# Expert stage: weight splits and gate products moved from GpSimd to VectorE, gates built by one float32 one-hot matmul per token

## The chip, the core and the metric

The kernel runs on one core of a Trainium2 chip. The metric is the device time of one execution in microseconds; shown is the median over several executions. The engines are called PE (TensorE's matmuls), DVE (VectorE), ACT (ScalarE), POOL (GpSimd) and SP (SyncE, which issues most of the transfers), as in the profile.

## The reference, cut to what matters

Two transformer blocks run one after the other over 512 tokens of width 1024. The second one ends in a feed-forward of 16384 experts, of which every token takes 16 in each of 8 heads. The change lies in this last part alone:

```python
def peer_ffn(x, wq, sub_keys, u_tab, v_tab):
    ...
    q = (xf @ wq).reshape(t, PEER_HEADS, 2, PEER_DKEY // 2)
    scores = jnp.einsum("thpc,hpnc->thpn", q, sub_keys).astype(jnp.float32)
    s_top, i_top = lax.top_k(scores, PEER_TOPK)
    cand_s = (s_top[:, :, 0, :, None] + s_top[:, :, 1, None, :]).reshape(t, PEER_HEADS, PEER_TOPK * PEER_TOPK)
    ...
    best_s, best_pos = lax.top_k(cand_s, PEER_TOPK)
    expert_idx = jnp.take_along_axis(cand_i, best_pos, axis=-1)
    gates = jax.nn.softmax(best_s, axis=-1)
    ...
        u = jnp.take(u_tab, ec, axis=0)
        act = jax.nn.gelu(jnp.einsum("cd,chkd->chk", xc, u).astype(jnp.float32)) * gc
        vv = jnp.take(v_tab, ec, axis=0)
        return jnp.einsum("chk,chkd->cd", act.astype(vv.dtype), vv)
```

An expert's number is i1 * 128 + i2, where i1 and i2 are places in two lists of 128 sub-keys.

## The kernel before

Everything is kept as [channel, token] tiles. A float32 product is made of three PE matmuls in the faster float32r type (`mm3`, L262 to L264): each operand is split into a high part, which ACT makes (`wh`, L249), and a low part, the difference, which is one subtraction on DVE or, if a caller says so, on POOL (`wl`, L250, in `unit`). A weight unit is [128, 1024] and comes by one transfer of 512 KB that SP issues (L246); there are four buffers for raw units and three for split ones.

`peer` does the expert stage. The experts of the first 128 tokens are gathered row by row: an indirect transfer that POOL issues (L1705), then one DVE instruction per row (L1689 for the dot product, L1697 for the weighted sum of the second table). For the other 384 tokens all 16384 experts are applied. The **first product** runs over 128 units of 128 experts, `j` in `range(NE)`: `proj` against the unit's columns of the first table (24 matmuls of 384 columns), then GELU on ACT (`hg`, L1758), then a transfer of the activations to DRAM (`HS`, L1759). In the units of the first product two generators are stepped in fixed rates: `route` (1.65 steps per unit) and `chosen`, the gathered rows. `route` first ranks: 16 query projections, scores against the sub-keys (plain float32 matmuls, L1576), the 16 largest by DVE (`top16`, L1506 to L1510), and `resolve`, which finds the sub-key numbers by one-hot products (equality on DVE at L1545, product on POOL at L1548, sum on DVE at L1551). Then it builds gates: for the 384 tokens, in six blocks of 64, four tokens at a time (96 such steps). Per step it makes a one-hot of i1 (`o1`, L1637) and of i2 (`o2`, L1639) on DVE and the i2 one-hot times the gate (`og`); a matmul per token multiplies them, and the [128 i1, 128 i2] result of each token goes from PSUM into `st`. Since the one-hot product is in float32r, the gate is split in two: `og` has a high half by ACT (four instructions, L1644) and a low half by POOL (L1641), the matmul has 256 columns (L1651), and the two halves are added as ACT copies the first into `st` (L1655) and DVE adds the second (L1656). A finished block goes to DRAM (`G`, L1669), the last stays in `st`.

The low half of the weights is made by POOL in every unit while the ranking is not done (`self.known < P`), and in every second one after that.

The **second product** has again 128 units, and `weighted(j)` prepares each: a weight unit of the second table, and for every pair of units the activations (`hs`, 384 KB, L1778) and gates (`gs`, 320 KB, L1780) from DRAM, both in tiles of the pool `four`, which has four. POOL multiplies them (`hg`, L1785 for the five blocks in `gs`, L1787 for the one in `st`), ACT and DVE split the product (`yh` L257, `yl` L258), and PE does 24 matmuls into eight PSUM banks. SP issues its transfers in one queue, in order; a transfer into a tile waits for the last reader of what was there.

A scheduler fixes each engine's order of instructions when the program is built; every engine then works through its own list, and an instruction that waits holds up all behind it.

## Time and profile before

| | |
|---|---|
| runs | 3840.15 us median of 3 (3839.1 to 3840.55) |
| span of the profiled execution | 3839.7 us |
| PE busy | 3588.0 us (93%) |
| DVE busy | 2635.3 us (69%) |
| ACT busy | 1529.3 us (40%) |
| POOL busy | 1204.1 us (31%) |
| granted PE clock, mean | 0.968 |

The profile is of one execution, and its span goes from the first to the last instruction; no other time of that execution is recorded, so the span is its own time here. An engine's busy time is the sum of its instructions' spans, and an instruction's span includes what it is held up by after it has started. The shares are means over a program of many stages. The expert stage is the last third: the first product from about 2430 us to 3264 us (ranking up to 2747 us, gates after that), the second from 3264 us to 3785 us.

### The profile page before, as it was taken

To read this page: it belongs to the slowest core of one execution; us is meant where nothing else is said; L and a number is where in the kernel's file an instruction comes from. 1 tells how busy PE (TensorE), PEld (TensorE's weight loads), DVE (VectorE), ACT (ScalarE), POOL (GpSimd) and SP (SyncE) were. 2 spreads that over 40 slices of the span, in tenths; PEclk is the share of its full clock that TensorE was granted. 3 is DMA by queue.
4 is the path that set the end of the run, shared out by engine and by line. 5 is a ranking of instruction groups with operands and counts; after the bars stand their busy time and mean duration, and the time that the engine had idled before them with its cause. 6 is when DMAs were issued, how large, how long until landed. Compare 5 with 4: busy or idle time off the path is not lost. (4 is left out here: it accounts for less than half of the span.)

```text
span 3839.7 us, 50675 instructions
## 1 busy us (share of the span) xinstructions
PE 3588.0 (93%) x18665; PEld 3119.2 (81%) x18665; DVE 2635.3 (69%) x4580; ACT 1529.3 (40%) x2746; POOL 1204.1 (31%) x987
## 2 busy tenths in 40 slices
PE   6999999999999999999999989899788888999996
PEld 4888876788888888767888877788788888999996
DVE  7555587655563324776332485689998999999997
ACT  3222366422232223564322353433356466333332
POOL 4000310100010002101000132466676676766664
PEclk9999999999999999999999999999899899999998
DMA  7566320266643333301333222476676777999994
GB/s 232 175 181 198 107 92 17 71 204 192 198 159 99 94 95 109 106 17 45 99 94 95 84 77 69 142 228 222 187 249 236 237 241 255 352 340 336 345 339 142
DMA packets 230329, 648.92 MB, mean 169 GB/s; under 512 B 22784, under 2 KB 80304, under 8 KB 227520
## 3 DMA queue, kind: packets, MB, share of 16 engines
q1 hardware_dynamic: 190592, 506.20, 40.6%
q0 software_dynamic: 39488, 139.48, 10.8%
q8 instruction: 146, 2.39, 0.3%
q14 instruction: 103, 0.84, 0.1%
HBM read 597.36 MB, written 48.23 MB: 168 GB/s over the span
## 5 line engine op out<-in xcount | busy, mean ns | idle before, releaser
L264 PE MATMUL proj<-yh,wl 128*128 128x512 f32 (+2 forms) x3296 | 1214.4, 370 | 52.9 <-DVE wl L250 33.7
L249 ACT ACTIVATE wh<-raw 128x1024 fp32r<-128x1024 f32 (+2 forms) x622 | 648.2, 1043 | 1446.8 <-PE proj L263 796.1
L262 PE MATMUL proj<-yh,wh 128*128 128x512 f32 (+2 forms) x3296 | 1204.3, 370 | 19.2 <-DVE cc L1455 8.8
L263 PE MATMUL proj<-yl,wh 128*128 128x512 f32 (+2 forms) x3296 | 1212.4, 369 | 7.9 <-DVE yl L380 3.9
L250 DVE TENSOR_TENSOR wl<-raw,wh 128x1024 fp32r<-128x1024 f32 (+2 forms) x527 | 707.3, 1343 | 500.8 <-ACT wh L249 495.5
L264 PEld LDWEIGHTS proj<-yh,wl 128*128 128x128 f32 x3296 | 635.4, 193 | 141.9 <-DVE wl L250 42.0
L262 PEld LDWEIGHTS proj<-yh,wh 128*128 128x128 f32 x3296 | 630.2, 193 | 107.9 <-DVE cc L1455 8.9
L263 PEld LDWEIGHTS proj<-yl,wh 128*128 128x128 f32 x3296 | 635.0, 193 | 92.9 <-DVE yl L380 7.3
L393 POOL TENSOR_TENSOR acc<-acc,sq 128x512 f32<-128x512 f32 x32 | 48.0, 1498 | 1482.2 <-ACT sq L392 1132.6
L262 PE MATMUL acc<-yh,wh 128*128 128x384 f32 x1024 | 344.5, 337 | 0.4 <-ACT yh L257 0.4
L263 PE MATMUL acc<-yl,wh 128*128 128x384 f32 x1024 | 344.4, 336 | 0.1
L264 PE MATMUL acc<-yh,wl 128*128 128x384 f32 x1024 | 343.9, 336 | 0.5 <-DVE wl L250 0.5
L264 PE MATMUL proj<-gh,wl 128*128 128x512 f32 (+1 forms) x792 | 293.2, 370 | 0.8 <-DVE wl L250 0.8
L262 PE MATMUL proj<-gh,wh 128*128 128x512 f32 (+1 forms) x792 | 292.9, 370 | 0.0
L263 PE MATMUL proj<-gl,wh 128*128 128x512 f32 (+1 forms) x792 | 292.8, 370 | 0.0
L250 POOL TENSOR_TENSOR wl<-raw,wh 128x1024 fp32r<-128x1024 f32 x95 | 240.8, 2538 | 100.3 <-ACT wh L249 99.7
L518 DVE SCALAR_TENSOR_TENSOR scr<-raw,cact 128x1024 bf16<-128x1024 f32 x128 | 161.9, 1265 | 160.6 <-DMA raw<-in_wada 160.0
L1705 POOL DMA_INDIRECT row<-in_purows,c x128 | 150.7, 1177 | 194.3 <-DVE row L1689 121.3
L1697 DVE SCALAR_TENSOR_TENSOR vacc<-row,act,vacc 128x1024 f32<-128x1024 f32 x127 | 208.8, 1644 | 0.4
L1689 DVE SCALAR_TENSOR_TENSOR row<-row,cact 128x1024 f32<-128x1024 f32 x128 | 196.7, 1549 | 11.0 <-DMA row<-in_purows,c 10.8
L1705 POOL DMA_INDIRECT row<-in_pv,c x128 | 149.9, 1171 | 158.3 <-DVE vacc L1697 69.7
L262 PEld LDWEIGHTS acc<-yh,wh 128*128 128x128 f32 x1024 | 192.4, 188 | 1.0 <-ACT yh L257 0.7
(432 smaller groups left out, 5176.6 us busy)
## 6 DMA issues: line engine op xcount, KB each, us to landing
raw<-in_wada SPq DMA_DIRECT2D x144, 512.0 KB
raw<-in_pu SPq DMA_DIRECT2D x128, 512.0 KB
raw<-in_pv SPq DMA_DIRECT2D x128, 512.0 KB
raw<-in_wg SPq DMA_DIRECT2D x84, 512.0 KB
raw<-in_wu SPq DMA_DIRECT2D x84, 512.0 KB
raw<-in_wd SPq DMA_DIRECT2D x64, 512.0 KB
acts<-hg SPq DMA_DIRECT2D x128, 192.0 KB
hs<-acts SPq DMA_DIRECT2D x64, 384.0 KB
```

The costliest lines, as they stand in the source:

```text
L249: nc.scalar.activation(h[:, :n], raw[:, :n], AF.Copy)
L250: ins = (engine or nc.vector).tensor_sub(l[:, :n], raw[:, :n], h[:, :n].bitcast(F32))
L262: mm(out, lhsT=lh, rhs=rh, start=start, stop=False)
L263: mm(out, lhsT=lh, rhs=rl, start=False, stop=False)
L264: mm(out, lhsT=ll, rhs=rh, start=False, stop=stop)
L393: (engine or nc.vector).tensor_add(acc[:, s], acc[:, s], sq)
L518: nc.vector.scalar_tensor_tensor(scr, raw, 1.0, self.cact, op0=OP.mult, op1=OP.mult, accum_out=self.mod[:, l, j:j + 1])
L1689: nc.vector.scalar_tensor_tensor(row, row, 1.0, XN, op0=OP.mult, op1=OP.mult, accum_out=a)
L1697: nc.vector.scalar_tensor_tensor(acc, row, a, acc, op0=OP.mult, op1=OP.add)
L1705: nc.gpsimd.indirect_dma_start(out=row, out_offset=None, in_=tables[kind], in_offset=bass.IndirectOffsetOnAxis(ap=self.experts[:GT, s:s + ...
```

## The change

Four edits, all in the expert stage:

- `unit` makes the low part of every weight of the first product on DVE.
- In `resolve` the one-hot product (L1548) goes from POOL to DVE.
- The gates are built from float32 one-hots without a split: `og` is one [128, 512] tile by four ACT instructions, the matmul per token is plain float32 of 128 columns, and one ACT instruction of 512 columns brings four tokens into `st`. The low half, its POOL product, the DVE addition and the split of the gates are gone. `og` now lies in the pool of 512-column tiles, no longer in `four`.
- In the second product ACT copies the last block's gates from `st` into `gs`, DVE makes the gate product in one instruction of 384 columns, and writes it over `hs`.

```diff
-                nc.gpsimd.tensor_tensor(e4, e4, it4[:, 2 * q:2 * q + 2, side, None, :].to_broadcast([P, 2, 16, 16]),
+                nc.vector.tensor_tensor(e4, e4, it4[:, 2 * q:2 * q + 2, side, None, :].to_broadcast([P, 2, 16, 16]),
                                         op=OP.mult)
...
-                gh = self.blk(F32R, name="gh")
-                self.split(tr[:, 2 * P:3 * P], gh[:, :P], gh[:, P:2 * P])
-                trb = gh[:, 2 * P:].bitcast(BF)[:, :P]
+                trb = tr[:, 384:].bitcast(BF)[:, :P]
...
-                o1, o2 = self.blk(F32R, name="o1"), self.tmp.tile([P, P, 4], BF, name="o2", tag="t", bufs=6)
-                og = self.four(F32R, "og").rearrange("p (a s b) -> p a s b", a=4, s=2)
+                o1, o2 = self.blk(name="o1"), self.tmp.tile([P, P, 4], BF, name="o2", tag="t", bufs=6)
+                og = self.blk(name="og")
...
-                ot = o2.rearrange("p e t -> p t e")
-                nc.gpsimd.tensor_tensor(og[:, :, 1], ot, ghf[:, P + q:P + q + 4, None].to_broadcast([P, 4, P]),
-                                        op=OP.mult)
                 for i in range(4):
-                    nc.scalar.activation(og[:, i, 0], ot[:, i], AF.Copy, scale=ghf[:, q + i:q + i + 1])
+                    nc.scalar.activation(og[:, i * P:(i + 1) * P], o2[:, :, i], AF.Copy,
+                                         scale=tr[:, 2 * P + q + i:2 * P + q + i + 1])
...
-                    for u in range(2):
-                        ps = self.bank("gp", "T")
-                        for i in range(2):
-                            v = u * 2 + i
-                            nc.tensor.matmul(ps[:, i * 256:(i + 1) * 256], lhsT=o1[:, v * P:(v + 1) * P],
-                                             rhs=og[:, v].rearrange("p a b -> p (a b)"), start=True, stop=True)
-                        p4 = ps.rearrange("p (t x e) -> p e t x", t=2, x=2)
-                        v = q - a + u * 2
-                        nc.scalar.activation(st[:, :, v:v + 2], p4[:, :, :, 0], AF.Copy)
-                        nc.vector.tensor_tensor(st[:, :, v:v + 2], st[:, :, v:v + 2], p4[:, :, :, 1], op=OP.add)
+                    ps = self.bank("gp", "T")
+                    for i in range(4):
+                        c = slice(i * P, (i + 1) * P)
+                        nc.tensor.matmul(ps[:, c], lhsT=o1[:, c], rhs=og[:, c], start=True, stop=True)
+                    nc.scalar.activation(st[:, :, q - a:q - a + 4], ps.rearrange("p (t e) -> p e t", t=4), AF.Copy)
...
-            ps = self.proj(A["pu"][j], dense, n=S - GT, engine=nc.gpsimd if self.known < P or j % 2 == 0 else None)
+            ps = self.proj(A["pu"][j], dense, n=S - GT)
...
             h, l = self.unit(A["pv"][:, j])
+            n, last = S - GT, len(BLOCKS) - 1
             if j % 2 == 0:
                 hs, g = self.four(F32, "hs"), self.four(F32, "gs")
-                n = 2 * (S - GT)
-                nc.sync.dma_start(hs[:, :n].rearrange("p (i t) -> p i t", i=2), HS[j // 2])
-                g4 = g[:, :(len(BLOCKS) - 1) * 2 * BT].rearrange("p (b i t) -> p b i t", i=2, t=BT)
-                nc.sync.dma_start(g4, G[:, :, j:j + 2])
+                nc.sync.dma_start(hs[:, :2 * n].rearrange("p (i t) -> p i t", i=2), HS[j // 2])
+                g4 = g[:, :2 * n].rearrange("p (b i t) -> p b i t", i=2, t=BT)
+                nc.sync.dma_start(g4[:, :last], G[:, :, j:j + 2])
+                nc.scalar.activation(g4[:, last], self.last_gates[:, j:j + 2], AF.Copy)
                 held["p"] = hs, g4
             hs, g4 = held["p"]
-            hg = self.blk(name="hg")[:, GT:]
-            c, e = (j % 2) * (S - GT), S - GT - BT
-            nc.gpsimd.tensor_mul(hg[:, :e].rearrange("p (b t) -> p b t", t=BT),
-                                 hs[:, c:c + e].rearrange("p (b t) -> p b t", t=BT), g4[:, :, j % 2])
-            nc.gpsimd.tensor_mul(hg[:, e:], hs[:, c + e:c + S - GT], self.last_gates[:, j])
+            hg = hs[:, (j % 2) * n:(j % 2 + 1) * n]
+            h3 = hg.rearrange("p (b t) -> p b t", t=BT)
+            nc.vector.tensor_mul(h3, h3, g4[:, :, j % 2])
```

What the scheduler makes of it stands in the engines' lists. The first place is DVE in the gate part of the first product; `o_` rows are the two one-hots, `wl` a weight's low part, `row` and `vacc` gathered rows, `st` the addition. Before:

```order
L1637 TENSOR_TENSOR o_24456<-pcst,tr 128x512
L250 TENSOR_TENSOR wl<-raw,wh 128x1024
L1689 SCALAR_TENSOR_TENSOR row,act<-row,cact 128x1024
L1656 TENSOR_TENSOR st<-st,gp 128x128x2 x2
L1639 TENSOR_TENSOR o_24457<-iota_19120,gh 128x512
L1637 TENSOR_TENSOR o_24513<-pcst,tr 128x512
L1656 TENSOR_TENSOR st<-st,gp 128x128x2 x2
L1689 SCALAR_TENSOR_TENSOR row,act<-row,cact 128x1024
```

and with the change:

```order
L1680 SCALAR_TENSOR_TENSOR row,act<-row,cact 128x1024
L1637 TENSOR_TENSOR o_24305<-iota_19120,tr 128x512
L1637 TENSOR_TENSOR o_24320<-iota_19120,tr 128x512
L1635 TENSOR_TENSOR o_24304<-pcst,tr 128x512
L250 TENSOR_TENSOR wl<-raw,wh 128x1024
L1635 TENSOR_TENSOR o_24319<-pcst,tr 128x512
L1680 SCALAR_TENSOR_TENSOR row,act<-row,cact 128x1024
```

The additions into `st` are gone, and a `wl` stands there for every unit, where before it was every second one.

The second place is DVE in the second product. Before, one round per unit:

```order
L1697 SCALAR_TENSOR_TENSOR vacc_19124<-row_32306,act_19386,vacc_19124 128x1024
L258 TENSOR_TENSOR yl_32530<-hg_32526,yh_32529 128x384
L250 TENSOR_TENSOR wl_32479<-raw_32476,wh_32478 128x1024
L1697 SCALAR_TENSOR_TENSOR vacc_19124<-row_32350,act_19386,vacc_19124 128x1024
L258 TENSOR_TENSOR yl_32574<-hg_32570,yh_32573 128x384
L250 TENSOR_TENSOR wl_32523<-raw_32520,wh_32522 128x1024
```

and with the change, one round per pair of units:

```order
L1777 TENSOR_TENSOR hs_31732<-hs_31732,gs_31733 128x384 x2
L250 TENSOR_TENSOR wl_31286<-raw_31283,wh_31285 128x1024
L1688 SCALAR_TENSOR_TENSOR vacc_19124<-row_31157,act_19386,vacc_19124 128x1024
L258 TENSOR_TENSOR yl_31615<-hs_31570,yh_31614 128x384
L250 TENSOR_TENSOR wl_31324<-raw_31321,wh_31323 128x1024
L1688 SCALAR_TENSOR_TENSOR vacc_19124<-row_31200,act_19386,vacc_19124 128x1024
L258 TENSOR_TENSOR yl_31658<-hs_31651,yh_31657 128x384
L1777 TENSOR_TENSOR hs_31813<-hs_31813,gs_31814 128x384 x2
L250 TENSOR_TENSOR wl_31367<-raw_31364,wh_31366 128x1024
L1688 SCALAR_TENSOR_TENSOR vacc_19124<-row_31238,act_19386,vacc_19124 128x1024
L258 TENSOR_TENSOR yl_31696<-hs_31651,yh_31695 128x384
```

Two products (L1777) now stand in DVE's list ahead of the pair's first `wl`. Of a pair's tile `hs`, which now holds the product, the last reader is the second `yl` of that pair: `hs_31570`, say, is free only after `yl_31615`. The tiles `hs_31651`, `hs_31732` and `hs_31813` are in use at that time, so of the four tiles of the pool it is this one into which `gs_31814` comes.

The third place is SP's queue in the second product. Before:

```order
L1778 DMA hs_31810<-acts_19117 128x768
L1780 DMA gs_31811<-gates_19116 128x5x128
L246 DMA raw_31764<-in_pv 128x1024
L246 DMA raw_31804<-in_pv 128x1024
L1778 DMA hs_31894<-acts_19117 128x768
```

and with the change:

```order
L1769 DMA hs_31732<-acts_19117 128x768
L246 DMA raw_31364<-in_pv 128x1024
L1771 DMA gs_31733<-gates_19116 128x5x128
L246 DMA raw_31402<-in_pv 128x1024
L1769 DMA hs_31813<-acts_19117 128x768
```

The two transfers of a pair no longer stand together: one weight unit is issued between them.

## Rows read from the trace of the kernel before

**Rows 1.** The page's 40 equal slices, busy tenths of VectorE and GpSimd.

```profile
DVE  7555587655563324776332485689998999999997
...
POOL 4000310100010002101000132466676676766664
```

**Rows 2.** Busy time by stage: ranking, gates, second product (us, PE, PEld, DVE, ACT, POOL, granted clock, DMA share, GB/s).

```profile
2430.00:2747.00 317.00, 279.21 (x1483) 259.29 (x1484) 274.44 (x1057) 107.84 (x150) 195.06 (x114) 0.96 0.67 212
2747.00:3264.00 517.00, 443.74 (x2431) 433.47 (x2430) 481.76 (x628) 302.95 (x759) 355.15 (x237) 0.92 0.72 241
3264.00:3785.00 521.00, 521.00 (x3006) 520.66 (x3005) 486.86 (x436) 198.85 (x255) 365.59 (x378) 1.00 0.97 337
```

**Rows 3.** Instructions by line, third matmul of the first product: ranking, then gates (eight per unit).

```profile
L264 PE MATMUL proj<-yh,wl 128*128 128x384 f32 x347 | 121.2, 349 | 31.2 <-DVE wl L250 18.4 <-POOL wl L250 12.8
...
L264 PE MATMUL proj<-yh,wl 128*128 128x384 f32 x678 | 240.2, 354 | 11.1 <-POOL wl L250 6.1 <-DVE wl L250 5.0
```

**Rows 4.** Instructions by line, first product, 2430 to 3264 us (busy us, mean ns | idle before).

```profile
L250 POOL TENSOR_TENSOR wl<-raw,wh 128x1024 fp32r<-128x1024 f32 x80 | 204.3, 2557 | 38.9 <-ACT wh L249 38.3
...
L1637 DVE TENSOR_TENSOR o<-pcst,tr 128x512 fp32r<-128x512 f32 x96 | 135.7, 1421 | 1.0 <-PE gp L1651 1.0
...
L1641 POOL TENSOR_TENSOR og<-o,gh 128x512 fp32r<-128x512 bf16 x96 | 121.0, 1270 | 30.3 <-DVE o L1639 27.6 <-PE gp L1651 1.8
...
L250 DVE TENSOR_TENSOR wl<-raw,wh 128x1024 fp32r<-128x1024 f32 x64 | 100.3, 1570 | 25.7 <-ACT wh L249 25.6
...
L1656 DVE TENSOR_TENSOR st<-st,gp 128x256 f32<-128x256 f32 x192 | 74.8, 435 | 8.4 <-ACT st L1655 8.4
...
L1548 POOL TENSOR_TENSOR eq<-eq,x 128x512 f32<-128x512 f32 x32 | 51.9, 1637 | 13.9 <-DVE eq L1545 13.7
```

**Rows 5.** Timeline of DVE, gates stage (start us, duration us).

```profile
2909.84 0.69 DVE L1637 TENSOR_TENSOR o<-pcst,tr 128x512 fp32r<-128x512 f32 x1
2910.45 3.02 DVE L1639 TENSOR_TENSOR o<-iota,gh 128x512 bf16<-128x512 bf16 x1
```

**Rows 6.** Timeline of POOL at the same time.

```profile
2910.80 2.37 POOL L250 TENSOR_TENSOR wl<-raw,wh 128x1024 fp32r<-128x1024 f32 x1
```

**Rows 7.** Timeline of PE, ranking stage: four code lines' float32 matmuls, and the next one.

```profile
2458.40 1.05 PE L1576 MATMUL sc<-keys,x 128*128 128x128 f32 x8
2459.21 0.42 PE L262 MATMUL proj<-yh,wh 128*128 128x384 f32 x1
```

**Rows 8.** Timeline of PE, gates stage: four gate matmuls of 256 columns, and the next one.

```profile
2923.23 0.65 PE L1651 MATMUL gp<-og,o 128*128 128x256 f32 x4
2923.71 0.33 PE L262 MATMUL proj<-yh,wh 128*128 128x384 f32 x1
```

**Rows 9.** Instructions by line, second product, 3264 to 3785 us.

```profile
L1785 POOL TENSOR_TENSOR hg<-hs,gs 128x320 f32<-128x320 f32 x126 | 155.4, 1233 | 0.1
...
L1787 POOL TENSOR_TENSOR hg<-hs,st 128x64 f32<-128x64 f32 x126 | 76.8, 609 | 2.6
```

**Rows 10.** Timeline of DVE, second product.

```profile
3507.52 1.21 DVE L1689 SCALAR_TENSOR_TENSOR row<-row,cact 128x1024 f32<-128x1024 f32 x1
...
3508.67 0.55 DVE L258 TENSOR_TENSOR yl<-hg,yh 128x384 fp32r<-128x384 f32 x1
3509.14 1.23 DVE L250 TENSOR_TENSOR wl<-raw,wh 128x1024 fp32r<-128x1024 f32 x1
3510.28 1.35 DVE L1689 SCALAR_TENSOR_TENSOR row<-row,cact 128x1024 f32<-128x1024 f32 x1
```

**Rows 11.** Timeline of SP, then POOL: the first transfer of `gs` and its first reader.

```profile
3252.46 0.61 SPq L1780 DMA_DIRECT2D gs<-gates  x1
...
3258.14 1.43 POOL L1785 TENSOR_TENSOR hg<-hs,gs 128x320 f32<-128x320 f32 x1 [4.37 <-DMA gs<-gates]
```

**Rows 12.** Timeline of SP, then ACT: a weight unit of an earlier, lightly loaded stage.

```profile
1542.50 0.33 SPq L246 DMA_DIRECT2D raw<-in_wint  x1
...
1546.13 1.06 ACT L249 ACTIVATE wh<-raw 128x1024 fp32r<-128x1024 f32 x1 [5.11 <-DMA raw<-in_wint]
```

More of the change, by code (lines that the diff above doesn't have):

```diff
@@ L1620, in route @@
                 nc.vector.tensor_copy(tr[:, :384], tp[:, :384])
-                gh = self.blk(F32R, name="gh")
-                self.split(tr[:, 2 * P:3 * P], gh[:, :P], gh[:, P:2 * P])
-                trb = gh[:, 2 * P:].bitcast(BF)[:, :P]
+                trb = tr[:, 384:].bitcast(BF)[:, :P]
                 nc.vector.tensor_copy(trb, tr[:, P:2 * P])
-                numbers[t] = tr, gh.bitcast(F32), trb
+                numbers[t] = tr, trb
                 yield
-            tr, ghf, trb = numbers[t]
+            tr, trb = numbers[t]
             st = self.stage.tile([P, NE, BT], F32, name="st", tag="st", bufs=1)
```

## Prediction

> **What bounds the kernel now.** I read the 40 slices first, then the busy times by stage, then the lines of each stage, and the timeline of two engines at one place. VectorE is busy for 90% or more in nearly all of the last third, and GpSimd for six to seven tenths there, while both are less busy earlier [rows 1]. The stages differ [rows 2]. In the second product PE is busy for 521.00 of 521 us at a granted clock of 1.00, so PE bounds it: 521/3006 = 0.173 us per matmul, 24 matmuls are 4.16 us per unit and 8.32 us per pair. In ranking and gates PE is idle for 38 and 73 us, and the granted clock is 0.96 and 0.92, that is, part of the time at 1.2 GHz after such gaps; there VectorE is busy for 274 of 317 and 482 of 517 us. What PE waits for there is a weight's low part, from VectorE or GpSimd [rows 3].
>
> Why VectorE is so busy is told by one place in the timeline. A one-hot (L1639) starts at 2910.45 and takes 3.02 us [rows 5]; GpSimd's split runs from 2910.80 for 2.37 us [rows 6], and VectorE ends 0.3 us after it. L1637 just before, with no GpSimd arithmetic beside it, took 0.69 us [rows 5], against a mean of 1421 ns [rows 4]. So arithmetic on GpSimd holds VectorE up, and an instruction moved from one to the other costs VectorE less than it seems.
>
> **First product, PE's side.** Ranking has 347/8 = 43.4 units, gates 678/8 = 84.7 [rows 3]. Ranking needs 43.4 × 4.16 = 181 us for units, 13 query units with 512 columns (three of 16 were begun before) at 0.173 × 512/384 = 0.231 us per matmul, so 13 × 24 × 0.231 = 72 us, and 16 × 0.81 = 13 us for scores: four float32 matmuls of the code are eight records that take from 2458.40 to 2459.21 [rows 7]. Sum 266 us. Gates need 84.7 × 4.16 = 352 us and 96 steps. A step is now four matmuls of 256 columns in 0.48 us [rows 8]; with the change it is four float32 ones of 128 columns, and I take the price of the scores, the same form: 0.81 us [rows 7]. So gates go from 352 + 46 = 398 to 352 + 78 = 430 us of PE work: the change **adds 32 us** to PE.
>
> **First product, VectorE's side.** Added are 80 splits [rows 4] at 1.14 us (start of one to start of the next [rows 10]) = 91 us, and 32 one-hot products (L1548 [rows 4]) for which I take 0.6 us, from L1637 with the same 512 elements (0.61 us from start to start [rows 5]) = 19 us. Removed are the additions, 74.8 us (L1656 [rows 4]). Removed too is the time that GpSimd holds VectorE up. At least that is what two lines show, 96 × (1421 − 690) = 70 us for L1637 and 64 × (1570 − 1230) = 22 us for L250 [rows 4, 5 and 10]; at most it is all of GpSimd's arithmetic, 204 + 121 + 52 = 377 us [rows 4]. I take 200: GpSimd's spans include its own waits for VectorE (a split of 2.37 us [rows 6] has a mean of 2557 ns), but three more VectorE lines must be stretched too. I give 60 of it to ranking, which has no gate products, and 140 to gates. Ranking then needs 274 + 40 × 1.14 + 16 × 0.6 − 60 = 270 us of VectorE beside 266 of PE: a tie, in which the two still wait for each other, and I take 290 us instead of 317. Gates need 482 + 40 × 1.14 + 16 × 0.6 − 75 − 140 = 322 us of VectorE beside 430 of PE: **PE becomes the bound**, and with 8% for gaps and clock (now it is 30%: 517 over 398) I take 465 instead of 517. The first product falls from 834 to 755 us, **−79**. Its ends: no gap at all, 266 + 430 = 696, −138; every gap as now, +32. ACT makes one eviction of 512 columns where it made two of 256, beside PE, for nothing; with PE as the bound, a late `og` would show next.
>
> **Second product.** GpSimd's products (155 + 77 us [rows 9]) become one of 384 columns per unit, and I price it as the split of 384 columns: 0.47 us from start to start [rows 10]. Per pair VectorE has two products, two weight splits, two rows and two splits: 2 × (0.47 + 1.14 + 1.15 + 0.47) = 6.5 us of 8.32. VectorE is not the bound, and PE can't go below 521 us. Nothing is gained here.
>
> But the change **adds a wait**. The product is now written over `hs`, so that tile stays taken until the pair's second low part. In the changed order, three pairs' tiles are in use, so the next `gs` is issued only after the second `yl` of a pair three back, and in VectorE's list that stands behind this pair's two products, a weight split and a row; the next products, which need that `gs`, stand one weight split, row and `yl` later. The round is therefore: two products, weight split, row and the whole `yl`, 2 × 0.47 + 1.14 + 1.15 + 0.55 = 3.78 us, and then the landing of `gs`. It decides where the landing takes over 8.32 − 3.78 = 4.54 us. From issue to its reader's start it took 3258.14 − 3252.46 = 5.68 us [rows 11]; a weight unit, 512 KB, in a light stage took 3.63 us [rows 12]. These are my bounds. I take 5.4, close to the first, since it is the same transfer: a round of 9.18 us, +0.86 per pair. The order has this pattern from the 14th pair to the 64th, 51 pairs: **+44 us** (from 0 to 58). What stands behind the waiting product on VectorE is the next weight split, for which PE waits. ACT's new copy into `gs` waits for the same `yl`, and is hidden behind the landing, which is longer than a copy and a weight's high part.
>
> By the Trainium skill's page DMA: Bandwidth & Descriptors, section Anatomy of one DMA, a transfer takes about 2.0 us plus its bytes over 436 GB/s, which for 320 KB is an estimate of 2.75 us; the trace's 5.68 us speaks against it, and by the page the 44 us would be 0.
>
> The sum: 3840.15 − 79 + 44 = **3805 us**. The profiled execution's span, 3839.7, is within 0.5 us of the median, so nothing is scaled.
>
> **The rivals.**
> - *The gates land in time.* Then PE bounds the second product as now, 3840 − 79 = 3761 us. For it: 3.63 us [rows 12], and a more even queue. Against it: rows 11, and a DMA share of 0.97 in that stage [rows 2]. The page named above would have it so.
> - *The landing is longer still, and the change is slower.* The same place; from 51 × (L − 4.54) = 79, so L = 6.1 us, it eats the gain. Rows 11 stand at the end of a stage with a DMA share of 0.72, the second product has 0.97 [rows 2]; 5.68 × 0.97/0.72 = 7.7 is the far end, halfway is 6.7, which gives +110 and 3871 us. Against it: a slower round asks for less.
> - *Gates gain little.* `og` and `o1` now share the 24-tile pool, of which 18 are always taken, so fewer steps are in flight and PE waits for `og`. If the first product gains 30 instead of 79, and the landing costs 44: 3854 us. For it: PE's own work grows by 32.
> - *The engines don't hold each other up, and VectorE is simply overfull.* Then nothing of the 200 us comes back, and gates need 322 + 140 = 462 and ranking 330 us of VectorE; with the 1.08 of above 855 us instead of 834, and 521 + 44 after it: 3905 us. The Trainium skill, Perfetto Trace Analysis, section Optimizing Scalar/DVE Operations, says that a saturated VectorE may be relieved by ScalarE or even GpSimd, which speaks against this change, and adds that the two share a read port, so that it might not help. Rows 5 and 6 side with the second half.
>
> **Chances.** The forecast 0.48 (its own range 3780 to 3835), gates in time 0.22, longer landing 0.15, gates gain little 0.11, overfull 0.04. The range 3745 to 3871 leaves out part of the longer landings, the overfull case and the best of the first product. A measurement of this kernel can tell about 0.2%, 7.7 us, from no change. Faster: nearly all of the forecast and all of the second case, 0.68; no difference: 0.08; slower: 0.24.
>
> **What would show it.** Mean spans of VectorE's lines back at their undisturbed size (L1637's twin near 0.69 us, splits near 1.22); in gates, PE busy near 95% and the clock above 0.92; 96 steps at 0.81 us. In the second product, VectorE's products waiting for `gs`, PE waiting for weight low parts, and a round near 9.2 us per pair. It is wrong if the second product stays at 521 us, if the gates stage stays above 490 us, or if VectorE's weight splits still have a mean far over 1.2 us.

## The result and the profile after

The changed kernel takes 3930.92 us (median of 4 runs, 3919.63 to 3941.16) beside 3839.81 us for the kernel before (3839.1 to 3840.55) on the same chip: a ratio of 1.0235 with a 95% interval of 1.0219 to 1.0252, 91 us slower. The prediction, 3805 us with a range of 3745 to 3871, was wrong, and on the wrong side.

The page of the changed kernel, its span and its busy times:

```profile
span 3917.9 us, 50838 instructions
PE 3636.2 (93%) x19049; PEld 3153.2 (80%) x19049; DVE 2420.4 (62%) x4625; ACT 1515.2 (39%) x2711; POOL 583.3 (15%) x523
```

POOL does half of what it did, and VectorE, which took its work over, is busy for less time than before (2420 us, 2635 before). So the change does what it says, and no engine is overfull. The windows by stage answer to [rows 2] (a border 5 us before the first `og`, as there; columns: busy time and instructions of PE, PEld, DVE, ACT and POOL, the granted clock, the DMA share and GB/s):

```profile
2430.00:2762.00 332.00, 289.51 (x1494) 266.67 (x1493) 282.10 (x1115) 110.24 (x151) 77.28 (x60) 0.95 0.61 201
2762.00:3206.00 444.00, 441.05 (x2810) 439.39 (x2809) 323.41 (x490) 293.80 (x663) 90.77 (x80) 1.00 0.82 282
3206.00:3862.00 656.00, 560.39 (x3006) 539.50 (x3005) 422.31 (x561) 193.50 (x318) 127.77 (x125) 0.96 0.82 267
```

Ranking went from 317 to 332 us, gates from 517 to 444 us, and the second product from 521 to 656 us for the same 3006 matmuls. The first product gained 58 us; the second lost 135. Nothing in the third row is at its limit: PE has 96 us without work (and its work itself takes 560 us for 521, at a granted clock of 0.96 where it was 1.00), VectorE is busy for 64% of the time, and the DMA share and rate fell from 0.97 and 337 GB/s to 0.82 and 267. That is the mark of a loop of waits. The chain of work that ended last, by engine and line, in shares of the span:

```profile
DMA gs<-gates 8%; PE proj L264 3%; PE proj L263 3%; PE proj L262 3%; DVE wl L250 2%; PE gp L1646 2%; DVE vacc L1688 1%; DVE row L1680 1%; DVE hs L1777 1%; DVE yl L258 1%; PE acc L264 1%; PE acc L262 1%; PE acc L263 1%; DVE eq L1545 0%; DVE eq L1548 0%
```

The largest item of the whole program is now one transfer of 320 KB per pair. One turn of the loop stands in three timelines from 3503 us on (columns: start, time, engine, line, operation; in brackets the idle time before and what ended it). SP first:

```profile
3509.68 0.33 SPq L1769 DMA_DIRECT2D hs<-acts  x1
3510.81 0.33 SPq L246 DMA_DIRECT2D raw<-in_pv  x1
3512.43 0.53 SPq L1771 DMA_DIRECT2D gs<-gates  x1
3514.98 0.34 SPq L246 DMA_DIRECT2D raw<-in_pv  x1
```

VectorE:

```profile
3508.62 1.03 DVE L1777 TENSOR_TENSOR hs<-hs,gs 128x384 f32<-128x384 f32 x2 [3.71 <-issue]
3509.57 1.22 DVE L250 TENSOR_TENSOR wl<-raw,wh 128x1024 fp32r<-128x1024 f32 x1
3510.70 1.22 DVE L1680 SCALAR_TENSOR_TENSOR row<-row,cact 128x1024 f32<-128x1024 f32 x1
3511.85 0.55 DVE L258 TENSOR_TENSOR yl<-hs,yh 128x384 fp32r<-128x384 f32 x1
...
3518.77 1.03 DVE L1777 TENSOR_TENSOR hs<-hs,gs 128x384 f32<-128x384 f32 x2 [2.21 <-DMA gs<-gates]
```

and POOL:

```profile
3512.20 1.02 POOL L1696 DMA_INDIRECT row<-in_purows,c  x1 [6.46 <-DVE row L1680]
```

The products start at 3508.62, and the `yl` that frees the tile ends at 3511.85 + 0.55 = 3512.40: 3.78 us, what the prediction put there. SP issues `gs` at 3512.43, and the next products start at 3518.77, 6.34 us later. VectorE stands still in that time, except for what it finds ahead of the products in its list. PE then waits for the split behind them: 95.6 us in the stage, all of it for VectorE's `wl`.

```profile
L264 PE MATMUL acc<-yh,wl 128*128 128x384 f32 x1000 | 353.0, 353 | 95.6 <-DVE wl L250 95.6
```

How long the transfers take, 3300 to 3780 us (count, KB each, median us from issue to landing):

```profile
raw<-in_pv SPq DMA_DIRECT2D x90, 512.0 KB, 5.1
hs<-acts SPq DMA_DIRECT2D x45, 384.0 KB, 3.3
gs<-gates SPq DMA_DIRECT2D x44, 320.0 KB, 6.9
```

`gs` is the smallest of the three and lands last: 6.9 us, where the prediction took 5.4.

### The profile page after: what moved, and what is told of

The parts are those of the page before. It is cut to its first block, busy times and chain, and to the rows that moved or that the text cites. A ratio compares the mean times of both kernels' runs of the same rounds, so it can differ in the third digit from the quotient of the medians.

```text
span 3917.9 us, 50838 instructions
## 1 busy us (share of the span) xinstructions
PE 3636.2 (93%) x19049; PEld 3153.2 (80%) x19049; DVE 2420.4 (62%) x4625; ACT 1515.2 (39%) x2711; POOL 583.3 (15%) x523
## 5 line engine op out<-in xcount | busy, mean ns | idle before, releaser
L264 PE MATMUL proj<-yh,wl 128*128 128x512 f32 (+2 forms) x3296 | 1197.6, 365 | 29.4 <-DVE wl L250 28.9
L250 DVE TENSOR_TENSOR wl<-raw,wh 128x1024 fp32r<-128x1024 f32 (+1 forms) x607 | 739.6, 1219 | 631.6 <-ACT wh L249 627.2
L264 PE MATMUL acc<-yh,wl 128*128 128x384 f32 x1024 | 361.0, 353 | 95.6 <-DVE wl L250 95.6
L262 PE MATMUL acc<-yh,wh 128*128 128x384 f32 x1024 | 354.1, 346 | 0.0
L263 PE MATMUL acc<-yl,wh 128*128 128x384 f32 x1024 | 354.0, 346 | 0.0
L264 PEld LDWEIGHTS acc<-yh,wl 128*128 128x128 f32 x1024 | 200.0, 195 | 116.6 <-DVE wl L250 114.0
L1696 POOL DMA_INDIRECT row<-in_purows,c x128 | 140.5, 1098 | 594.2 <-DVE row L1680 340.8
L1696 POOL DMA_INDIRECT row<-in_pv,c x128 | 140.7, 1099 | 525.3 <-DVE vacc L1688 309.9
L263 PEld LDWEIGHTS acc<-yl,wh 128*128 128x128 f32 x1024 | 199.6, 195 | 0.0
L264 PEld LDWEIGHTS proj<-gh,wl 128*128 128x128 f32 x792 | 151.2, 191 | 28.0 <-DVE wl L250 2.4
```

The lines of the kernel that those rows point to most:

```text
L250: ins = (engine or nc.vector).tensor_sub(l[:, :n], raw[:, :n], h[:, :n].bitcast(F32))
L262: mm(out, lhsT=lh, rhs=rh, start=start, stop=False)
L263: mm(out, lhsT=lh, rhs=rl, start=False, stop=False)
L264: mm(out, lhsT=ll, rhs=rh, start=False, stop=stop)
L1696: nc.gpsimd.indirect_dma_start(out=row, out_offset=None, in_=tables[kind], in_offset=bass.IndirectOffsetOnAxis(ap=self.experts[:GT, s:s + ...
```

## The experiments

Theory: the loop of `gs` is the loss, and its size is set by the landing. Rivals: VectorE's products, too few tiles, rows pushed into the second product.

### Is it the loop?

**A tile of its own** for the product, still on VectorE:

```diff
-            hg = hs[:, (j % 2) * n:(j % 2 + 1) * n]
-            h3 = hg.rearrange("p (b t) -> p b t", t=BT)
-            nc.vector.tensor_mul(h3, h3, g4[:, :, j % 2])
+            hg = self.blk(name="hg")[:, GT:]
+            h3 = hs[:, (j % 2) * n:(j % 2 + 1) * n].rearrange("p (b t) -> p b t", t=BT)
+            nc.vector.tensor_mul(hg.rearrange("p (b t) -> p b t", t=BT), h3, g4[:, :, j % 2])
```

> The changed kernel, but the gate product is written to a tile of its own instead of over hs, so that hs and gs are both free as soon as the product has read them. Theory (the loop): the loss comes from gs being issued only after the second yl of a pair three back, and then 6.9 us of landing, a round of some 10.7 us per pair against 8.3 us of PE work. With the tile of its own the wait is for a product that lies several instructions further back, so the second product should come back to 521 to 540 us: the time is about 3918 - 134 = 3785 us (3775 to 3800). Rival (VectorE): the products, 128 of 0.5 us, are now on VectorE and simply cost too much there; nothing of that is changed here, so the time stays at 3920 to 3930 us.

Measured: 3792.7 us, ratio to before 0.9879 (0.986 to 0.9898). Its second product:

```profile
3205.00:3726.00 521.00, 520.97 (x3005) 520.36 (x3004) 420.80 (x558) 197.94 (x319) 128.90 (x125) 1.00 0.97 337
```

PE is full again, with the products on VectorE and VectorE as busy as in the changed kernel (421 us). The loss is the tile that stays taken, and none of it is VectorE's work.

**Five tiles** instead of four:

```diff
-        return self.stage.tile([P, 1024], dt, name=name, tag="four", bufs=4)
+        return self.stage.tile([P, 768], dt, name=name, tag="four", bufs=5)
```

> The changed kernel with five tiles for hs and gs instead of four (each of 768 columns instead of 1024, which is what they use). Theory (the loop): the order lets VectorE's products run ahead as far as there are tiles, so with five tiles gs waits for the second yl of a pair four back instead of three back, and between that yl and the product that needs gs there are still only one weight split, one row and one yl in VectorE's list. The round stays at 3.8 us plus the landing, the time at 3900 to 3940 us. Rival (too few tiles): one more tile takes the wait away, and the time is 3785 us.

Measured: 3926.98 us, 1.0215 (1.0195 to 1.0236), as slow as the change. A further buffer alone gives nothing, since the order of VectorE's list uses it up to place the products one pair earlier: at 3512 us VectorE has started 69 products and 63 `yl`, in the changed kernel 70 and 66.

**The old second product** in the changed kernel (`weighted` word for word as before):

```diff
-            nc.vector.tensor_mul(h3, h3, g4[:, :, j % 2])
+            nc.gpsimd.tensor_mul(hg[:, :e].rearrange("p (b t) -> p b t", t=BT),
+                                 hs[:, c:c + e].rearrange("p (b t) -> p b t", t=BT), g4[:, :, j % 2])
+            nc.gpsimd.tensor_mul(hg[:, e:], hs[:, c + e:c + S - GT], self.last_gates[:, j])
```

> The changed first product (weight splits and one-hot products on VectorE, float32 gates) with the second product as it was before (gate products on GpSimd, in a tile of their own). Theory: the first product alone gains what the trace of the change shows, 832 to 774 us, and the second product is as before: 3840 - 55 = 3785 us, first product near 775 us. Rival: the first product is faster only because work was pushed into the second one (gathered rows), and the second product comes out longer than 537 us by some of the 55: 3800 to 3840 us.

Measured: 3789.14 us, 0.9866 (0.9849 to 0.9882). **The new second product alone**, the reverse exchange in the kernel before:

> The kernel before with the changed second product alone. Theory (the loop): it has nothing to do with the first product, so the loss stands by itself: 3840 + 134 = 3974 us (3955 to 3990), second product near 671 us. Rival: the loss hangs on the rows that the faster first product left for the second; then it is clearly smaller here, 3840 to 3900 us.

Measured: 3981.15 us, 1.0355 (1.0335 to 1.0376). So the first product is worth -51.5 us by itself and the second +140; their sum, +89, is near the change's +91. So the parts hardly act on each other.

### Why does it land so late?

Six more kernels have the same loop with another landing. In each, I took the mean interval between two issues of the transfer in the loop (the round of a pair) and the mean time from its issue to the start of the product that reads it (the landing), from 3330 to 3760 us:

| kernel | in the loop | round, us | landing, us | difference |
|---|---|---|---|---|
| the change | `gs` | 10.70 | 6.89 | 3.81 |
| five tiles | `gs` | 11.02 | 7.20 | 3.82 |
| new second product alone | `gs` | 10.93 | 7.10 | 3.83 |
| gates in one piece | `gs` | 9.37 | 5.57 | 3.80 |
| gates first | `hs` | 9.18 | 5.33 | 3.85 |
| gates by ACT | `gs` | 11.36 | 7.47 | 3.89 |
| first and in one piece | `hs` | 10.17 | 6.30 | 3.87 |
| half weights | `gs` | 9.31 | 5.47 | 3.84 |
| no rows | `gs` | 8.29 | 4.47 | 3.82 |

The difference is 3.80 to 3.89 us in all nine, and the prediction had 3.78. In the last kernel PE is full, and the round is PE's own 8.3 us; there many products don't wait for `gs`, so that 4.47 us is the most that the landing can be. The form of the loop is right; what was wrong is the landing.

**Gates in one piece** per partition, 2560 bytes instead of five times 512:

```diff
-        G = self.dram.tile([P, len(BLOCKS) - 1, NE, BT], F32, name="gates")
+        G = self.dram.tile([P, NE // 2, len(BLOCKS) - 1, 2, BT], F32, name="gates")
...
-                nc.sync.dma_start(g4[:, :last], G[:, :, j:j + 2])
+                nc.sync.dma_start(g4[:, :last], G[:, j // 2])
```

> The changed kernel, with the gates laid out in DRAM so that gs comes as one piece of 2560 bytes per partition (128 packets) instead of five of 512 bytes (640 packets). The order of instructions and the wait for the yl stay. Both theories take the loop as given and ask why gs lands so late (6.9 us, where hs with more bytes lands in 3.3 us). Theory (pieces): the packets of 512 bytes take turns one for one with the 4096-byte packets of the gathered rows, so gs needs 40 turns per transfer engine instead of 8; with big pieces it lands in 4 to 5 us, the round is 8.3 to 8.8 us per pair, and the time is 3790 to 3820 us. Rival (place): gs lands late because it is issued behind hs and a weight unit in the same queue; the pieces change nothing, landing 6 to 7 us, time 3890 to 3930 us.

Measured: 3863.43 us, 1.0058 (1.0041 to 1.0075), landing 5.57 us: between the two theories. Writing the gates in small pieces made the first product some 12 us longer.

**Gates first**:

```diff
-                hs, g = self.four(F32, "hs"), self.four(F32, "gs")
-                nc.sync.dma_start(hs[:, :2 * n].rearrange("p (i t) -> p i t", i=2), HS[j // 2])
+                g, hs = self.four(F32, "gs"), self.four(F32, "hs")
                 g4 = g[:, :2 * n].rearrange("p (b i t) -> p b i t", i=2, t=BT)
                 nc.sync.dma_start(g4[:, :last], G[:, :, j:j + 2])
+                nc.sync.dma_start(hs[:, :2 * n].rearrange("p (i t) -> p i t", i=2), HS[j // 2])
```

> The changed kernel with gs allocated and issued before hs. Now hs takes the tile that waits for the yl of the pair three back, at the same place in VectorE's list, and gs takes the one that is free early; so hs, in packets of 3072 bytes, is the transfer in the loop. Theory (pieces): hs lands faster than gs did, in 4 to 5 us, and the time is 3790 to 3830 us. Rival (place): whatever stands last, behind the other one and a weight unit, lands late; hs takes 6 to 7 us from its issue and the time is 3890 to 3930 us.

Measured: 3837.59 us, 0.9994 (0.9982 to 1.0006), landing of `hs` 5.33 us, again between the two theories; where it stood first it was 3.3. So the place in the queue counts, with pieces of 3072 bytes too.

**Gates by ACT**, in ACT's own queue:

```diff
-                nc.sync.dma_start(g4[:, :last], G[:, :, j:j + 2])
+                nc.scalar.dma_start(g4[:, :last], G[:, :, j:j + 2])
```

> The changed kernel with gs issued by ACT, in a queue of its own, instead of by SP behind hs and the weight units. ACT issues it where its copy into gs already waited for the same yl, so the loop is otherwise the same. Rival (place): without hs and raw ahead of it, gs starts at once and lands in 4 to 5 us, round 8.3 to 8.8 us per pair, time 3790 to 3820 us. Theory (pieces): the 640 packets still take turns with rows and now with the weight units too, landing 6 us or more, time 3890 to 3930 us or worse.

Measured: 3971.79 us, 1.0349 (1.0332 to 1.0367), landing 7.47 us. Another queue doesn't help.

**First and in one piece**, both edits together:

> The changed kernel with both edits on the transfer: gs first and in pieces of 2560 bytes. hs is in the loop (5.3 us when it stood behind gs in 512-byte packets). Theory (pieces, also for what stands behind): with 128 packets of gs ahead instead of 640, hs lands in about 4.5 us, the round is 8.3 us, the second product 537 to 550 us; with the 12 us that the small writes of the gates cost the first product, 3800 to 3815 us. Rival (place): hs lands late because a weight unit stands just ahead of it; 5.3 us as before, second product near 588 us, time 3845 to 3855 us. In both, the round less the landing should be 3.8 us, as in the other runs.

Measured: 3893.43 us, 1.0128 (1.0089 to 1.0168), landing of `hs` 6.30 us. Neither theory had that. What the theory of the pieces says of a transfer that stands behind is refuted: with 128 packets ahead instead of 640, it landed later, not sooner. For `gs` itself the size of the pieces does count (5.57 us for 6.89), but it is not the whole cause, and nor is the place in the queue, so I looked at what else flies. POOL's row of 512 KB is issued at 3512.20, 0.23 us ahead of `gs` (timeline above), because the same stretch of VectorE's list frees both.

**No rows** in the second product:

```diff
+            if self.still is None:
+                row = self.stage.tile([P, D], F32, name="row", tag="row", bufs=ROWS)[:GT]
+                nc.gpsimd.indirect_dma_start(out=row, out_offset=None, in_=tables[kind],
...
+                last = row
+            else:
+                row = last
```

> The changed kernel, whose second product issues no transfers of gathered rows: VectorE's instructions on rows stay, but all read the last row that came in the first product, so the first 128 tokens are not computed. The loop in the lists is the same. Theory (rows): gs is stretched by a row of 512 KB that POOL issues within half a microsecond of it, and whose 4096-byte packets take turns with those of gs; without rows gs lands in 4 to 4.5 us, the round is 8.3 us or less, and PE bounds the second product again: 3785 to 3800 us. Rival (weight unit): gs is late because of the weight unit and hs that stand 1.6 and 2.8 us ahead of it in the same queue; then it still takes 5.5 us or more and the time is 3850 us or more. In both, round less landing should be 3.8 us as long as the loop decides.

**Half weights**:

```diff
-            h, l = self.unit(A["pv"][:, j])
+            h, l = self.half_unit(A["pv"][:, j])
...
+        nc.sync.dma_start(raw[:, :512], src[:, :512])
+        r = raw[:, None, :512].to_broadcast([P, 2, 512])
```

> The changed kernel, whose second product loads only the first half of each weight unit (256 KB instead of 512) and splits it twice, so that ACT, VectorE and PE do the same work on half the weights. Rows stay. Theory (rows): gs starts some 0.7 us sooner after its issue, but the row still takes turns with its 640 packets: landing about 6 us, time 3870 to 3900 us. Rival (weight unit): with half the bytes ahead gs lands in 4.5 to 5 us, time 3800 to 3830 us.

Measured: no rows 3786.71 us, 0.9855 (0.9838 to 0.9871), landing 4.47 us, as the theory of the rows had it; half weights 3853.05 us, 1.0024 (1.001 to 1.0038), landing 5.47 us, between the two theories. Without rows, SP and VectorE show, from 3509 us on:

```profile
3509.15 0.53 SPq L1781 DMA_DIRECT2D gs<-gates  x1
```

```profile
3513.91 1.03 DVE L1787 TENSOR_TENSOR hs<-hs,gs 128x384 f32<-128x384 f32 x2 [0.58 <-DMA gs<-gates]
```

4.76 us, hardly more than the loop forgives. Without the rows at least 2.4 of the 6.9 us are gone, and with half of each weight unit 1.4. Each of the two edits takes bytes from the whole stage, so how much of this is the one row and the one weight unit that leave just ahead of `gs`, and how much the load in general, is not shown. What the timelines show is that the transfers freed by one turn of the loop leave together, and the one in the loop is the last of them.

The Trainium skill, DMA: Bandwidth & Descriptors, section Queues, rings and completion order, says that each transfer engine goes round the queues it has work for and drains a batch of descriptors from one before it turns to the next; the two runs above agree with it, and no run here shows the size of a batch. The same page, section Issuing engines are not separate DMA queues, says that starting transfers from several engines saves only issue time; the run with ACT agrees (7.47 us).

### Where the first product's gain comes from

**Splits only** (the kernel before, with `engine=` taken out of the call of `proj`):

```diff
-            ps = self.proj(A["pu"][j], dense, n=S - GT, engine=nc.gpsimd if self.known < P or j % 2 == 0 else None)
+            ps = self.proj(A["pu"][j], dense, n=S - GT)
```

> The kernel before with one edit: all weight splits of the first product on VectorE. Everything else stays on GpSimd and in float32r halves. Theory: the ranking gets slower as in the change (by some 10 us), and in the gates, where VectorE was already busy for 482 of 517 us, 40 more splits cost 46 us that the lighter GpSimd gives back only in part; the time is 3840 to 3860 us. Rival: the hold-up by GpSimd is the main thing, and without its splits the gates come out faster by most of the 70 us: 3780 to 3800 us.

Measured: 3803.98 us, 0.9892 (0.9875 to 0.9908). The theory fell, and the time is close to the rival's. Its ranking and gates, and two of VectorE's lines in the gates:

```profile
2435.00:2772.00 337.00, 294.98 (x1511) 274.41 (x1510) 278.43 (x1106) 111.72 (x154) 109.02 (x76) 0.93 0.61 200
2772.00:3232.00 460.00, 420.87 (x2396) 412.80 (x2395) 434.12 (x656) 300.11 (x754) 254.49 (x193) 0.96 0.77 268
```

```profile
L250 DVE TENSOR_TENSOR wl<-raw,wh 128x1024 fp32r<-128x1024 f32 x85 | 125.0, 1472 | 6.4 <-ACT wh L249 6.4
L1637 DVE TENSOR_TENSOR o<-pcst,tr 128x512 fp32r<-128x512 f32 x92 | 82.4, 901 | 4.4 <-PE gp L1651 4.4
```

VectorE makes 40 splits more than before (85 for 45) and is busy for 48 us less (434 for 482): 40 splits cost it 40 × 1.22 = 49 us, so GpSimd's 40 must have held it up by some 49 + 48 = 97 us, nearly twice that. This is an estimate, and some 3 us too high: four of the 96 one-hots of L1637 lie ahead of this window. Ranking got longer, as in the change.

**Gates only** (the kernel before with float32 one-hots, its splits left on GpSimd):

```diff
-                gh = self.blk(F32R, name="gh")
-                self.split(tr[:, 2 * P:3 * P], gh[:, :P], gh[:, P:2 * P])
...
+                og = self.blk(name="og")
...
+                        nc.tensor.matmul(ps[:, c], lhsT=o1[:, c], rhs=og[:, c], start=True, stop=True)
```

> The kernel before with one edit: the gates from float32 one-hots without halves, that is, without the gate split, GpSimd's low half and VectorE's addition (96 steps). Splits stay as before. Theory: this is where the 70 us of the gates come from: VectorE loses 75 us of additions and GpSimd 121 us, and PE, with 32 us more to do, becomes the bound; ranking as before, gates near 450 us, time 3770 to 3785 us. Rival: it takes both edits; alone it gives half or less, 3800 to 3830 us.

Measured: 3791.85 us, 0.9861 (0.9845 to 0.9878): the gates came out as the theory had them, the time 7 us above its range. Its gates:

```profile
2760.00:3213.00 453.00, 439.17 (x2765) 437.07 (x2766) 343.62 (x422) 288.51 (x656) 232.69 (x138) 0.99 0.79 271
```

Alone the edits take 57 and 64 us off the gates (460 and 453 us for 517), together 73: the second to come finds PE as the bound, busy for 441 of 444 us in the change. In the time of the whole kernel, the gates alone already give all that the changed first product gives: 0.9861 here and 0.9866 for the run with the old second product, which has the moved splits and one-hot products as well. What these add in the gates (453 to 444 us) goes again in the ranking.

**Ranking's splits back on GpSimd**, in the kernel with a tile of its own:

```diff
-            ps = self.proj(A["pu"][j], dense, n=S - GT)
+            ps = self.proj(A["pu"][j], dense, n=S - GT, engine=nc.gpsimd if self.known < P else None)
```

> The kernel of the run with a tile of its own (3793 us), but while the sub-keys are ranked the weight splits stay on GpSimd as before; while the gates are built they are on VectorE as in the change. In the change the ranking took 332 us (317 before) and the gates 444 us (517 before). Theory: moving the splits is a loss in the ranking, where VectorE's short sorting steps stand ahead of each split and PE waits for the weight's low part, and a gain in the gates; with the splits of the ranking back on GpSimd it returns to about 317 us and the time to 3778 us (3770 to 3785). Rival: the ranking is slower through the one-hot products of L1548 on VectorE, or through the order; then it stays near 332 us and the time at 3793 us, or GpSimd's splits hold VectorE up and it gets worse.

Measured: 3776.56 us, 0.9835 (0.9818 to 0.9851), the fastest of all, 16 us under its base. The first `og` comes 323 us after the first matmul of the first product, as in the kernel before, and 335 us in the change. **Ranking's one-hot product back on GpSimd** as well (L1548):

```diff
-                nc.vector.tensor_tensor(e4, e4, it4[:, 2 * q:2 * q + 2, side, None, :].to_broadcast([P, 2, 16, 16]),
+                (nc.gpsimd if self.known < P else nc.vector).tensor_tensor(e4, e4, it4[:, 2 * q:2 * q + 2, side, None, :].to_broadcast([P, 2, 16, 16]),
```

> The kernel with a tile of its own and the ranking's splits on GpSimd (3777 us), and in the ranking the one-hot product of L1548 on GpSimd again too, so that the ranking is as before. The ranking already takes 323 us there, as before. Theory: the 16 instructions of 0.7 us weigh nothing, and time is the same, 3773 to 3781 us. Rival: they hold GpSimd and VectorE up, 3782 us or more.

Measured: 3780.12 us, 0.9836 (0.982 to 0.9853): no difference.

## Why the prediction was wrong

**The step that failed is the landing of `gs`.** "I take 5.4, close to the first, since it is the same transfer." It was 6.89 us, above the 6.1 that the prediction gave as the point where the gain is eaten. [rows 11] showed a time under the old order: there `hs`, a weight unit, `gs` and a row were issued over 5.0 us (`hs` at 3247.81, the row at 3252.78). The change made the waits release the same four within 2.8 us, and so changed the number that was read. Two runs show the landing of `gs` in a second product with PE full and a DMA share of 0.97: first the run with splits only, which has the old second product and issues `gs` some 2.5 us behind `hs`; then the run with the ranking's one-hot product back on GpSimd, which has the product in a tile of its own and issues `hs` and `gs` within 0.4 us, just behind a row. At the end of each line stands the median from issue to landing, from 3300 to 3780 us:

```profile
gs<-gates SPq DMA_DIRECT2D x52, 320.0 KB, 5.6
gs<-gates SPq DMA_DIRECT2D x49, 320.0 KB, 7.5
```

So 5.4 was near the truth for the old order, even at full load; in the kernels whose issues stand closer together, the landing is longer. In the second of the two runs that costs nothing (PE is full). The 2.75 us that the prediction took from the Trainium skill's page DMA: Bandwidth & Descriptors, section Anatomy of one DMA, was further off still; the fit there was measured on transfers that GpSimd issues, and SP issues `gs`.

The argument against the longer landing, "a slower round asks for less", did not hold: the DMA share did fall, 0.97 to 0.82, but the transfer in the loop still flies in the crowded part of each round. With the measured landing, the prediction's own formula gives 51 × (6.89 - 4.54) = +120 us, where +44 was taken; the first and last matmul of the stage show +134 (537 to 671 us), and what makes up the other 14 stays open.

**The rival that came true** was the second, the longer landing, at its place and in the same loop: 0.15 was too little. Its size came out by luck. It scaled the landing by the DMA share, and the lines speak against that: the same share of 0.97 stands with 5.6 us and with 7.5, and the change has 6.89 us at 0.82. That its halfway point (6.7 us) and far end (7.7) bracket what was measured shows nothing. Its 3871 us were 60 short of 3931: some 27 because it too carried the -79, and some 30 because the second product lost 140 us for its 110.

**First product, -79.** It gained 51.5 us (run with the old second product). Gates went better than forecast: VectorE needed 323.41 us (322 predicted), PE's work was 441 us (430 predicted; a step took 0.85 us for 0.81, which is 4 of the 11) and the stage 444 us for 465, at a clock of 1.00. By the prediction's own prices, some 190 of the 200 us for which GpSimd held VectorE up came back, 141 in the gates and 48 in the ranking (an estimate); since the 200 was picked between 92 and 377, part of that is luck. Ranking failed: 332 us for 290. VectorE's own time there, 282 us, was near the 270 of the sum. PE's was 289.51 us for 266: the sum went by the full clock, and the 279.21 us before [rows 2] were already above it at a granted clock of 0.96. PE's gaps were 42.5 us, where the forecast left 24 for gaps and clock together; what it left out is that a split on VectorE brings its wait with it. VectorE's line of splits in the ranking of the changed kernel:

```profile
L250 DVE TENSOR_TENSOR wl<-raw,wh 128x1024 fp32r<-128x1024 f32 x58 | 72.7, 1255 | 53.7 <-ACT wh L249 53.7
```

Now 58 splits wait for 53.7 us, with the sorting steps behind them, and PE stands for 25.0 us for the low part and 17.5 for GELU:

```profile
L262 PE MATMUL proj<-yh,wh 128*128 128x384 f32 (+1 forms) x454 | 166.3, 366 | 17.5 <-ACT hg L1749 17.5
L264 PE MATMUL proj<-yh,wl 128*128 128x384 f32 (+1 forms) x453 | 164.2, 365 | 25.0 <-DVE wl L250 25.0
```

In the same stage of the kernel before, 19 splits waited for 11.6 us, and PE stood for 37.8 us for the low part and not for GELU:

```profile
L250 DVE TENSOR_TENSOR wl<-raw,wh 128x1024 fp32r<-128x1024 f32 x19 | 26.1, 1380 | 11.6 <-ACT wh L249 11.6
L264 PE MATMUL proj<-yh,wl 128*128 128x384 f32 (+1 forms) x451 | 162.9, 361 | 37.8 <-DVE wl L250 25.0 <-POOL wl L250 12.8
```

So PE's gaps grew by less than 5 us over the kernel before, where the forecast had them shrink. That the moved splits make the ranking longer is shown by the run that puts them back (335 to 323 us); that it is their wait in VectorE's list is argued from these lines.

**What was right.** GpSimd's arithmetic holds VectorE up: the one-hot of i1 fell from 1421 ns [rows 4] to 901 where nothing but the splits was moved (run with splits only), and in the gates of the changed kernel to 687, the split to 1237. The place in [rows 5] was an extreme one: the mean of L1639 fell only from 656 ns to 426. The changed kernel's lines:

```profile
L250 DVE TENSOR_TENSOR wl<-raw,wh 128x1024 fp32r<-128x1024 f32 x86 | 106.4, 1237 | 63.0 <-ACT wh L249 62.9
L1635 DVE TENSOR_TENSOR o<-pcst,tr 128x512 f32<-128x512 f32 x95 | 65.3, 687 | 48.0 <-PE gp L1646 47.8
```

The overfull rival is out, and the rule of the Trainium skill (Perfetto Trace Analysis, section Optimizing Scalar/DVE Operations) that work moved between these two might not help, since they share a read port, agrees here in the other direction: with the work back on VectorE, that engine is busy for less time. That `og` and `o1` share a pool did no harm: the 48 us that VectorE idles for PE there lie in a stage in which PE waits for under 3 us. And the round of 3.78 us plus landing held in the eight kernels in which the loop sets it.

The better version follows from this: the changed gates and their splits, the product on VectorE in a tile of its own, and the ranking's splits on GpSimd: 3776.56 us, 65 us under the kernel before as run beside it (3842.0 us), a ratio of 0.9835.

## What to carry to other kernels

A result written over its input keeps the input's buffer until its last reader; where a transfer waits for that buffer, the round is the instructions from the product to that reader plus the landing, and another buffer doesn't help if the engine's order runs one step further ahead. Don't price such a transfer by its landing in the old order: the new order decides what leaves beside it, so ask what else the same turn releases. And where an engine takes over work with a wait in front, count the wait in its list along with the work.

## What the runs showed of the hardware

- A transfer's landing does not follow its size here: in the changed kernel 320 KB of `gs` land after 6.9 us and 384 KB of `hs` after 3.3. The 512-byte packets of `gs` have a mean of 28.5 ns in the trace's packet records, so 640 of them are 640 × 28.5 / 16 = 1.14 us on 16 transfer engines, yet it lands after 6.9 us beside gathered rows and behind a weight unit, and after 4.47 us at most without rows.
- A queue of its own made it later (7.47 us), and large packets ahead made what came behind later, not sooner (6.30 us for 5.33). Why the last, stays open.
- Forty GpSimd subtractions of 128x1024 cost VectorE more than 90 us of longer spans (an estimate from the run with splits only), most of their own length (41 of them took 108.2 us in that stage before). VectorE's search for the largest sub-keys was not held up: L1507 had 282 ns in the ranking before, and 290 in the changed kernel.
- A plain float32 matmul of 128 columns is two records; 16 records, that is eight tokens, took 1.70 us from start to the next matmul's start (2900.11 to 2901.81), 0.85 us per four tokens.
